# A two-layer decoder trunk on one core: where the token statistics are transposed, and when the relative-bias table is made

## The chip, the cores and the metric

The kernel runs on 1 core of one Trainium2 chip. The metric is device time in microseconds (us); the kernel before takes 1341.06 us, the median of 3 runs (1340.65 to 1341.84).

## The reference

512 tokens of width 1024 pass through two layers. In short:

```python
hn = rmsnorm(h, norm_mix_g[i])
h = h + mixer(hn)            # layer 0: stick-breaking and differential heads; layer 1: dilated attention
h = h + square(relu(rmsnorm(h, norm_mlp_g[i]) @ w_mlp_up[i])) @ w_mlp_down[i]
h = h + (p[i] @ w_ple_proj[i]) * sigmoid(rmsnorm(h, norm_ple_g[i]) @ w_ple_gate[i])
```

Two parts of the mixers matter here. `rmsnorm` divides each token by the root of its mean square, so every query, key and value of a token carries one factor for that token. And the softmax heads (the differential ones of layer 0 and all of layer 1) add a bias that depends on the distance of query and key alone: `table[t5_bucket(rel)]`, from a table of 32 buckets by 16 heads.

## The kernel before, in words

**Tiling.** The activations lie transposed, as eight tiles `h[k]` of 128 features by 512 tokens. Every fp32 operand is split into a high and a low part, and each product is three matmuls (`mm3`, lines 129 to 131). ScalarE (ACT) makes the high part of weights (L120); GpSimd (POOL) or VectorE (DVE) makes the low part (L121).

**One mixer.** Heads come in four groups; layer 0 takes them in the order 2, 3, 0, 1, the first two being differential heads. `project(g)` (L389) makes a group's queries, keys and values. For the first group of a layer (`start`) it runs `queries_keys()` and then `values()`; for later groups the values come first. `attend` (L529) runs in steps that `interleave` (L150) places between the units of the next group's `project`.

**The first group.** Queries are contracted first (two accumulators, "mm" banks of PSUM), then key block 0 (an "mm" bank) and key block 1 (an "sc" bank). After key block 0 `statistics()` (L373) finishes the token statistics: two matmuls with a matrix of ones (L237, L238), then `rsqrt` (L192) on ACT and DVE, whose last step (L199) gives `rstd`, a tile that holds each token's factor along its columns. `tok_cols` (L257) turns it into one column per 128 tokens: four transposes on TensorE (PE; L260) and one DVE instruction (L262) that writes `rcol`. Then the held queries and the keys are evacuated (`evacuate`, L448): each takes one DVE product with `rstd` (L451) into the single "tmp" buffer, ACT copies (L457, L465, L466) and DVE differences (L458, L467). `values()` fills two PSUM banks, one "sc" and one "tp", with 96 matmuls in two halves, and `evacuate_values` (L412) scales them by `rcol` (ACT L421, DVE L422).

**The table.** `prepare()` (L301) is called once, after the first `project` of layer 0 (L625). It takes four "e" tiles and the "tmp" tile, loads the table, a 0/1 matrix and offsets by six transfers (L304 to L309) and the lambda vectors by one (L312, into "tmp"), multiplies the table in two pieces (PE L316, each into a fresh one of the two "sc" banks), joins the offsets (four DVE instructions, L318) and writes the result to device memory (`urow`, four transfers, L319). Five small DVE and ACT instructions (L320 to L325) make the lambda factor. `load_bias` (L488) reads `urow` (L491) at the start of a differential head or a dilated head, and `soft` (L494) adds it to the scores by a DVE instruction (L499).

**What sets the order.** The program text gives each instruction its dependencies and its rank; the order on each engine's queue is fixed at build time by a planner, which lets an engine take the highest-ranked instruction that it holds to be ready. So an engine's order differs from the text: the transposes (L260), which the text puts ahead of key block 1, stand in the trace between that block's 17th and 18th matmul, and the loads of the next group (L112) stand ahead of the table's. At run time each queue keeps that order and waits where an operand is late.

Of the kernel before, what the change touches and what calls it, by code (L numbers as in the profile page):

```python
# [62 lines left out]
def trunk(  # L63
# [8 lines left out]
    def nm(s):  # L72
        uid[0] += 1
        return f"{s}_{uid[0]}"
# [13 lines left out]
    def t2k(tag, pool=None, dtype=F32):  # L88
        return (pool or spool).tile([P, S], dtype, tag=tag, name=nm(tag), bufs=T_BUFS.get(tag, 2))
# [6 lines left out]
    def ps(tag):  # L96
        return psum.tile([P, S], F32, tag=tag, name=nm(tag), bufs=PS_BUFS[tag])
# [4 lines left out]
    def ps_wide():  # L102
        t = ps(wide[wide_i[0] % 8])
        wide_i[0] += 1
        return t
# [4 lines left out]
    def wload(src):  # L110
        raw = wpool.tile([P, src.shape[-1]], F32, tag="raw", name=nm("raw"), bufs=2)
        nc.sync.dma_start(raw, src)  # L112
        return raw

    def wsplit(raw, i, nk, n, pool=None):
        bufs = 3 if pool is None else 4
        hi = (pool or wpool).tile([P, nk, n], F32R, tag="wh", name=nm("wh"), bufs=bufs)
        lo = (pool or wpool).tile([P, nk, n], F32R, tag="wl", name=nm("wl"), bufs=bufs)
        src = raw[:, i * nk * n:(i + 1) * nk * n].rearrange("p (k c) -> p k c", k=nk)
        nc.scalar.activation(hi, src, AF.Copy)  # L120
        lo_eng[0].tensor_tensor(lo, src, hi.bitcast(F32), op=ALU.subtract)  # L121
        return hi, lo

    def block(src, nk, n):
        raw = wload(src)
        return [wsplit(raw, i, nk, n) for i in range(src.shape[-1] // (nk * n))]

    def mm3(acc, lh, ll, rh, rl, start, stop):
        nc.tensor.matmul(acc, lh, rh, start=start, stop=False)  # L129
        nc.tensor.matmul(acc, lh, rl, start=False, stop=False)  # L130
        nc.tensor.matmul(acc, ll, rh, start=False, stop=stop)  # L131
# [69 lines left out]
    def use_tables(after):  # L201
        ins = nc.scalar.preload_act_table_set("natural_log_exp_and_others").ins
        for a in after:
            order(ins, a)
        return ins
# [51 lines left out]
    def tok_cols(rstd):  # L257
        rp = ps("tp")
        for t in range(QT):
            nc.tensor.transpose(rp[:, t * P:(t + 1) * P], rstd[:, t * P:(t + 1) * P], ident)  # L260
        rc = spool.tile([P, QT], F32, tag="rcol", name=nm("rcol"), bufs=2)
        nc.vector.tensor_scalar(rc, rp.rearrange("p (t c) -> p t c", c=P)[:, :, 0], -0.5, None, op0=ALU.mult)  # L262
        return rc
# [96 lines left out]
    def mixer(layer, norm, nxt):  # L360
# [10 lines left out]
        stat = {}  # L371

        def statistics():  # L373
            if not layer:
                for k in range(KT):
                    norm.stats(k, last_split)
            stat["rstd"] = norm.finish(use_tables(sig_tail) if layer else None)
            stat["rcol"] = tok_cols(stat["rstd"])

        nblk = [0]  # L380

        def next_block():
            nblk[0] += 1
            return w_in[layer, nblk[0] - 1]
# [4 lines left out]
        def project(g, cur):  # L389
            kind = "dil" if layer else ("sb" if g < 2 else "diff")  # L390
            start = not first
            first.append(g)
            v = mpool.tile([P, QT, 512], F32R, tag="v", name=nm("v"), bufs=2)

            def values():
                raw = wload(next_block())
                banks = [ps_wide() if start else ps("mm") for _ in range(QT // 2)]
                accs = [b[:, c:c + 256] for b in banks for c in (0, 256)]
                for half in range(2):
                    wh, wl = wsplit(raw, half, 4, 256)  # L400
                    for t in range(QT):
                        for k in range(4):
                            ah, al = ahl[4 * half + k]
                            tk = slice(t * P, (t + 1) * P)
                            mm3(accs[t], ah[:, tk], al[:, tk], wh[:, k], wl[:, k],
                                half == 0 and k == 0 and t % 2 == 0, half == 1 and k == 3 and t % 2 == 1)
                            yield 1.0
                        if half == 1 and t % 2 == 1:
                            evacuate_values(t - 1, accs[t - 1])
                            evacuate_values(t, accs[t])  # L410

            def evacuate_values(t, acc):  # L412
                sc = stat["rcol"][:, t:t + 1]
                if kind == "diff":
                    src = acc
                    vh, vl = v[:, t, 0:256], v[:, t, 256:512]
                else:
                    src = acc.rearrange("p (a c) -> p a c", a=4)
                    vv = v[:, t, :].rearrange("p (a b c) -> p a b c", a=4, b=2)
                    vh, vl = vv[:, :, 0, :], vv[:, :, 1, :]  # L420
                nc.scalar.activation(vh, src, AF.Copy, scale=sc)  # L421
                nc.vector.scalar_tensor_tensor(vl, src, sc, vh.bitcast(F32), op0=ALU.mult, op1=ALU.subtract)  # L422

            heads = []

            def queries_keys():
                qscale = -0.5 * HD ** -0.5 if kind == "sb" else 0.5 * HD ** -0.5
                qk, waiting = [], []
                for isq in (True, False):
                    src = next_block()  # L430
                    lo_eng[0] = nc.vector if start else nc.gpsimd
                    blk = blk0 if isq and start and not layer else block(src, KT, P)
                    lo_eng[0] = nc.gpsimd
                    accs = [ps_wide() if start else ps("mm") for _ in range(2)]
                    if start and isq:
                        yield from lin_units(accs, blk, ahl, 0, KT, True)
                        waiting = accs
                        continue
                    for i, acc in enumerate(accs):
                        yield from lin_units([acc], [blk[i]], ahl, 0, KT, False)  # L440
                        if waiting:
                            statistics()
                            for x, held in enumerate(waiting):
                                evacuate(True, x, held, qk, qscale)
                            waiting = []
                        evacuate(isq, i, acc, qk, qscale)

            def evacuate(isq, i, acc, qk, qscale):  # L448
                rstd = stat["rstd"]
                f = t2k("tmp")  # L450
                nc.vector.scalar_tensor_tensor(f, acc, qscale if isq else -0.5, rstd, op0=ALU.mult, op1=ALU.mult)  # L451
                lower, upper = slice(0, 64), slice(64, 128)
                if isq:
                    qq = []
                    for a, b in ((lower, upper), (upper, lower)):
                        q = mpool.tile([P, S], F32R, tag="qq", name=nm("qq"), bufs=6)
                        nc.scalar.activation(q[a], f[a], AF.Copy)  # L457
                        nc.vector.tensor_tensor(q[b], f[a], q[a].bitcast(F32), op=ALU.subtract)  # L458
                        qq.append(q)
                    qk.append(qq)  # L460
                else:
                    for s, (a, b) in enumerate(((lower, upper), (upper, lower))):
                        kl = klz[s][kl_i[0] % KLB]
                        kh = mpool.tile([P, S], F32R, tag="kh", name=nm("kh"), bufs=5)
                        nc.scalar.activation(kh[a], f[a], AF.Copy)  # L465
                        nc.scalar.activation(kh[b], f[a], AF.Copy)  # L466
                        nc.vector.tensor_tensor(kl[a], f[a], kh[a].bitcast(F32), op=ALU.subtract)  # L467
                        heads.append((qk[i][s], kh, kl))
                    kl_i[0] += 1
            cur.extend((g, kind, v, heads))  # L470
            if start:
                wide_i[0] = 0
                yield from queries_keys()
                yield from values()
            else:
                yield from values()
                yield from queries_keys()
# [144 lines left out]

        cur = []
        run(project(groups[0], cur))
        if layer == 0:  # L625
            prepare()
        for n, g in enumerate(groups[1:]):
            steps = attend(*cur)
            cur = []
# [253 lines left out]
```

## Time and profile before

| | |
|---|---|
| Median of 3 runs | 1341.06 us (1340.65 to 1341.84) |
| Profiled execution | 1337.92 us, span 1336.1 us |
| PE busy | 1300.5 us, 97% of the span |
| DVE busy | 817.4 us, 61% |
| ACT busy | 632.2 us, 47% |
| POOL busy | 164.4 us, 12% |
| Mean granted clock of PE | 0.998 |

Busy time is the union of an engine's instructions. PE's is near the whole span, but matmuls overlap in the pipe, so what it could save is read from its waits and from the chain of work that ended last. The span is 1.8 us shorter than the execution's own time, which is 3.14 us under the median.

### The profile page before, as it was taken

How to read it: one execution, taken by the hardware profiler on the slowest of the kernel's cores; microseconds unless marked ns; L12 is line 12 of the kernel's file. 1: busy time of each engine (PE TensorE's matmuls, PEld its weight loads, DVE VectorE, ACT ScalarE, POOL GpSimd, SP SyncE). 2: the span in 40 equal slices, each digit the busy share in tenths (PEclk: the TensorE clock that was granted, in tenths of full speed). 3: DMA queues.
4: the chain of work that ended last, by engine and by line, in shares of the span. 5: the costliest groups of instructions: out<-in, count | busy, mean ns of one | idle time of the engine just before them, and what ended most of it. 6: DMA issues, size and time to landing. Idle time of an engine off the chain costs nothing.

```text
span 1336.1 us, 16330 instructions
## 1 busy us (share of the span) xinstructions
PE 1300.5 (97%) x6360; PEld 1088.8 (81%) x6360; DVE 817.4 (61%) x1389; ACT 632.2 (47%) x1085; POOL 164.4 (12%) x90
## 2 busy tenths in 40 slices
PE   8999999899999999999999999999999999999997
PEld 6878777688888888888888898888888888888886
DVE  6788789865344344345667888887644434434566
ACT  5576758554223232233456666775422313324344
POOL 2322332310000000000003222221000000000001
PEclk9999999999999999999999999999999999999999
DMA  6321322243233222222232232213322232322221
GB/s 217 109 89 56 119 87 103 88 158 98 101 104 104 98 95 95 95 95 95 95 119 87 76 112 74 72 64 133 119 95 95 98 103 103 105 96 95 95 79 64
DMA packets 28030, 133.06 MB, mean 100 GB/s; under 512 B 3312, under 2 KB 4048, under 8 KB 15280
## 3 DMA queue, kind: packets, MB, share of 16 engines
q1 hardware_dynamic: 27952, 132.01, 29.0%
q8 instruction: 50, 0.82, 0.2%
q14 instruction: 28, 0.23, 0.1%
HBM read 125.63 MB, written 6.37 MB: 99 GB/s over the span
## 4 chain that ended last, share of the span: by engine, by line
PE 75%; DVE 14%; ACT 7%; issue 2%; DMA 0%; SPq 0%; ACTq 0%
PE mm L130 11%; PE mm L129 11%; PE mm L131 11%; PE tp L129 5%; PE tp L131 5%; PE tp L130 5%; PE sc L129 5%; PE sc L131 5%; PE sc L130 5%; PE pv L130 2%; PE pv L129 2%; PE pv L131 2%; DVE qq L458 2%; DVE e L563 2%; PE pv L525 2%
## 5 line engine op out<-in xcount | busy, mean ns | idle before, releaser
L120 ACT ACTIVATE wh<-raw 128x1024 fp32r<-128x1024 f32 (+1 forms) x216 | 224.7, 1043 | 496.8 <-PE mm L130 178.4
L129 PE MATMUL mm<-hi,wh 128*128 128x512 f32 x564 | 226.2, 401 | 0.5 <-ACT hi L169 0.5
L130 PE MATMUL mm<-lo,wh 128*128 128x512 f32 x564 | 220.5, 391 | 0.6 <-DVE lo L170 0.6
L131 PE MATMUL mm<-hi,wl 128*128 128x512 f32 x564 | 220.4, 391 | 0.3 <-DVE wl L121 0.3
L121 DVE TENSOR_TENSOR wl<-raw,wh 128x1024 fp32r<-128x1024 f32 x150 | 183.4, 1224 | 44.1 <-ACT wh L120 37.8
L121 POOL TENSOR_TENSOR wl<-raw,wh 128x1024 fp32r<-128x1024 f32 (+1 forms) x66 | 153.8, 2331 | 348.7 <-ACT wh L120 320.6
L131 PEld LDWEIGHTS mm<-hi,wl 128*128 128x128 f32 x564 | 105.9, 188 | 23.4 <-DVE wl L121 0.8
L129 PEld LDWEIGHTS mm<-hi,wh 128*128 128x128 f32 x564 | 106.2, 188 | 21.3 <-ACT hi L169 1.3
L130 PEld LDWEIGHTS mm<-lo,wh 128*128 128x128 f32 x564 | 106.2, 188 | 20.2 <-DVE lo L170 1.3
L502 ACT ACTIVATE e<-e,mn 128x128 f32<-128x128 f32 (+3 forms) x96 | 53.9, 561 | 51.5 <-DVE mn L499 50.8
L130 PE MATMUL mm<-ul,wh 128*128 128x512 f32 x192 | 74.7, 389 | 0.0
L131 PE MATMUL mm<-uh,wl 128*128 128x512 f32 x192 | 74.7, 389 | 0.0
L129 PE MATMUL mm<-uh,wh 128*128 128x512 f32 x192 | 74.7, 389 | 0.0
L131 PE MATMUL sc<-hi,wl 128*128 128x512 f32 x168 | 65.6, 390 | 0.0
L130 PE MATMUL sc<-lo,wh 128*128 128x512 f32 x168 | 65.4, 389 | 0.0
L129 PE MATMUL sc<-hi,wh 128*128 128x512 f32 x168 | 65.4, 389 | 0.0
L129 PE MATMUL mm<-wh,hi 128*128 128x256 f32 (+1 forms) x216 | 65.4, 303 | 0.0
L130 PE MATMUL mm<-wl,hi 128*128 128x256 f32 (+1 forms) x216 | 64.1, 297 | 0.4 <-DVE wl L121 0.4
L131 PE MATMUL mm<-wh,lo 128*128 128x256 f32 (+1 forms) x216 | 63.8, 295 | 0.0
L675 DVE TENSOR_TENSOR h<-h,mm 128x512 f32<-128x512 f32 x24 | 16.5, 688 | 72.7 <-PE mm L131 72.7
L129 PE MATMUL tp<-hi,wh 128*128 128x512 f32 x152 | 59.1, 389 | 0.0
L130 PE MATMUL tp<-lo,wh 128*128 128x512 f32 x152 | 59.1, 389 | 0.0
(218 smaller groups left out, 2835.1 us busy)
## 6 DMA issues: line engine op xcount, KB each, us to landing
raw<-in_w_up_dram SPq DMA_DIRECT2D x32, 1024.0 KB, 4.9
raw<-in_w_down_dram SPq DMA_DIRECT2D x32, 1024.0 KB, 4.9
raw<-in_w_in_dram SPq DMA_DIRECT2D x23, 1024.0 KB, 4.9
raw<-in_w_gate_dram SPq DMA_DIRECT2D x8, 1024.0 KB, 4.9
bias<-urow SPq DMA_DIRECT2D x24, 256.0 KB, 3.2
raw<-in_w_outa_dram SPq DMA_DIRECT2D x8, 768.0 KB, 4.3
pjd<-tmp SPq DMA_DIRECT2D x16, 256.0 KB, 2.2
pj<-pjd SPq DMA_DIRECT2D x16, 256.0 KB, 4.8
```

Source lines behind the costliest of these rows:

```text
L120: nc.scalar.activation(hi, src, AF.Copy)
L121: lo_eng[0].tensor_tensor(lo, src, hi.bitcast(F32), op=ALU.subtract)
L129: nc.tensor.matmul(acc, lh, rh, start=start, stop=False)
L130: nc.tensor.matmul(acc, lh, rl, start=False, stop=False)
L131: nc.tensor.matmul(acc, ll, rh, start=False, stop=stop)
L458: nc.vector.tensor_tensor(q[b], f[a], q[a].bitcast(F32), op=ALU.subtract)
L502: nc.scalar.activation(e[:, 0:n], e[:, 0:n], AF.Exp, scale=-1.0, bias=mn, accum_out=s)
L525: nc.tensor.matmul(op[:, q0:S], stat(j), mov, start=c == 0, stop=c == nmm - 1)
L563: nc.vector.tensor_tensor_scan(kr, kr, kr, 1.0, op0=ALU.mult, op1=ALU.bypass)
L675: nc.vector.tensor_tensor(h[2 * c + i], h[2 * c + i], acc, op=ALU.add)
```

## The change

Three edits. `tok_cols` leaves `statistics()` and is called in `values()` of a layer's first group, when the second half of the value weights has been split and before that half's matmuls (in both layers). `prepare()` leaves its place after the first `project` and is called in that `project` of layer 0, between `queries_keys()` and `values()`. No instruction is added or taken away.

```diff
@@ statistics
             stat["rstd"] = norm.finish(use_tables(sig_tail) if layer else None)
-            stat["rcol"] = tok_cols(stat["rstd"])
@@ values
                 for half in range(2):
                     wh, wl = wsplit(raw, half, 4, 256)
+                    if start and half == 1:
+                        stat["rcol"] = tok_cols(stat["rstd"])
                     for t in range(QT):
@@ project
                 yield from queries_keys()
+                if not layer:
+                    prepare()
                 yield from values()
@@ mixer
         run(project(groups[0], cur))
-        if layer == 0:
-            prepare()
         for n, g in enumerate(groups[1:]):
```

## Rows read from the trace of the kernel before

**Rows 1.** The page: busy time of each engine with its share of the span, and the shares of the chain that ended last by engine.

```profile
PE 1300.5 (97%) x6360; PEld 1088.8 (81%) x6360; DVE 817.4 (61%) x1389; ACT 632.2 (47%) x1085; POOL 164.4 (12%) x90
...
PE 75%; DVE 14%; ACT 7%; issue 2%; DMA 0%; SPq 0%; ACTq 0%
```

**Rows 2.** PE's waits over the whole span: engine, tile and line that waited, the instruction that ended the wait, then us in total, times, longest.

```profile
PE sc L484 <- DVE mn L499: 5.0, 4, 1.8
...
PE tp L260 <- DVE rstd L199: 3.2, 2, 2.0
PE sc L316 <- DVE v L422: 1.9, 1, 1.9
...
PE sc L484 <- DVE v L422: 0.9, 1, 0.9
```

**Rows 3.** The chain that ended last, layer 0, from the statistics to the second group's values: start us, us, what.

```profile
30.96 0.70 DVE rstd L199
31.69 0.70 DVE tmp L451
32.41 0.64 ACT qq L457
33.08 0.69 DVE qq L458
...
46.08 0.69 DVE klz L467
46.81 0.49 DVE v L422
...
47.83 0.49 DVE v L422
48.37 0.39 PE sc L316 x2
```

**Rows 4.** The timeline of PE around the transposes of layer 0 and around the table's products: start us, us, engine, line, operation, out<-in, count, and in brackets the idle time before and what ended it.

```profile
29.29 0.39 PE L130 MATMUL sc<-lo,wh 128*128 128x512 f32 x1
31.71 0.66 PE L260 MATMUL tp<-ident,rstd 128*128 128x128 f32 x4 [2.03 <-DVE rstd L199]
32.12 0.48 PE L131 MATMUL sc<-hi,wl 128*128 128x512 f32 x1
...
45.41 1.03 PE L316 MATMUL sc<-e,e 32*16 32x512 f32 x2
...
48.69 0.39 PE L129 MATMUL mm<-wh,hi 128*128 128x256 f32 x1
```

**Rows 5.** The same place in layer 1: two pieces of the chain, then four rows of PE's timeline.

```profile
706.30 0.70 DVE tmp L451
...
722.45 0.50 DVE v L422
...
704.81 0.39 PE L130 MATMUL sc<-lo,wh 128*128 128x512 f32 x1
706.33 0.65 PE L260 MATMUL tp<-ident,rstd 128*128 128x128 f32 x4 [1.13 <-DVE rstd L199]
...
721.87 0.28 PE L131 MATMUL mm<-wh,lo 128*128 128x256 f32 x1
723.08 0.36 PE L484 MATMUL sc<-kh,qq 128*128 128x256 f32 x1 [0.93 <-DVE v L422]
```

**Rows 6.** The timeline of DVE, layer 0.

```profile
32.40 0.16 DVE L262 TENSOR_SCALAR rcol<-tp 128x4 f32<-128x4 f32 x1
...
42.14 0.69 DVE L451 SCALAR_TENSOR_TENSOR tmp<-sc,rstd 128x512 f32<-128x512 f32 x1
...
48.62 1.27 DVE L318 SCALAR_TENSOR_TENSOR e<-sc,e 16x512 f32<-16x512 f32 x2
...
50.21 0.47 DVE L318 SCALAR_TENSOR_TENSOR e<-sc,e 16x128 f32<-16x128 f32 x2
...
55.18 0.29 DVE L499 CUSTOM_DVE_ANT_0 e<-sc,bias 128x128 f32<-128x128 f32 x1 [2.51 <-PE mm L131]
```

**Rows 7.** The queue of SP, layer 0; then the landing time of the 0/1 matrix's load (KB each, median us from issue to landing) and of the first three loads of the bias.

```profile
30.53 0.41 SPq L305 DMA_DIRECT2D e<-in_onehot_dram  x1
...
46.84 0.35 SPq L312 DMA_DIRECT2D tmp<-in_lambdas_dram  x1
...
51.88 1.29 SPq L491 DMA_DIRECT2D bias<-urow  x3
...
e<-in_onehot_dram SPq DMA_DIRECT2D x1, 64.0 KB, 5.3
...
DMA to landing us min/median/max: 3.2/3.5/3.6
```

**Rows 8.** Busy time by stretch: us, then each engine's busy us and instructions, the granted clock of PE, the DMA share and GB/s.

```profile
29.30:32.10 2.80, 0.77 (x6) 0.40 (x5) 2.70 (x4) 0.00 (x0) 0.35 (x1) 1.00 0.52 120
45.40:48.70 3.30, 1.37 (x6) 0.23 (x5) 2.70 (x6) 1.94 (x5) 0.10 (x1) 1.00 0.62 194
60.00:75.00 15.00, 15.00 (x86) 12.51 (x85) 13.15 (x45) 11.52 (x29) 5.05 (x2) 1.00 0.29 100
75.00:130.00 55.00, 50.38 (x291) 43.18 (x289) 47.05 (x112) 36.45 (x80) 14.96 (x7) 1.00 0.23 70
1330.00:1333.00 3.00, 0.00 (x0) 0.00 (x0) 1.90 (x6) 2.27 (x6) 0.00 (x0) 0.55 0.40 157
```

## The prediction, made before the changed kernel was run

> **What bounds the kernel now.** I read the page first: PE is busy 97% of the span, but the chain that ended last runs on PE for 75%, on DVE for 14% and on ACT for 7% [rows 1]. So there are stretches where PE works and yet does not set the end, and a wait of PE in such a stretch is worth nothing by itself. Then PE's waits: the transposes wait for the statistics twice, 3.2 us in total, and the table's second product waits 1.9 us [rows 2]. These two are what the change touches. Last the chain through that place: the reader is to see that from `rstd` (done at 31.66) it goes through DVE and ACT, query by query and key by key, to the second value evacuation (47.83 to 48.32), and comes back to PE only at the table's second product, 48.37 [rows 3]. The transposes are not on it. Layer 1 has the same chain, from the first evacuation at 706.30 to the second value evacuation at 722.45; there PE waits 0.93 us for that very instruction [rows 5].
>
> **The change part by part.**
>
> *The transposes, layer 0.* PE stops after the matmul of 29.29; matmuls follow each other there every 0.23 us, so the next could start at 29.52 and starts at 32.12: 2.60 us, 2.03 of it idle and 0.41 the transposes themselves [rows 4]. Without them key block 1 (7 matmuls left, 1.6 us) ends at 31.2 instead of 33.8. The 96 value matmuls fill 33.8 to 45.41, 0.12 us each, 11.6 us together; with the 0.41 of the transposes put back among them they end at 31.2 + 11.6 + 0.41 = 43.2. The transposes then find `rstd` long done, so no wait replaces the old one. But the values' evacuation needs ACT and DVE, and these stand in the chain above until 46.81 whatever PE does [rows 3]. The DVE instruction that moves along (0.16 us at 32.40) lies in a gap in which DVE waits for ACT's copy, 32.41 to 33.05 [rows 3, 6]. **Worth on the end: 0**, bounds 0 and -0.16.
>
> *The transposes, layer 1.* The same: the next matmul could start at 705.04 and starts at 706.74 (transposes at 706.33, 0.41 us), so PE gains 1.70 - 0.41 = 1.29 us. It then meets the wait at 723.08, which ends with the DVE chain: 0.93 becomes 2.2 us [rows 5]. Worth 0, same bounds.
>
> *The table: what is queued where.* Its loads stand on SP's queue from 30 us, already ahead of the values' work, because SP takes what is ready, not what the text lists first; the 0/1 matrix lands at 30.53 + 5.3 = 35.83 [rows 7]. The value weights were loaded before that, so I expect none of these to move, and SP to hold nothing back. The lambda load needs the single "tmp" buffer, so it stays behind the last key difference (46.77), at 46.84; what queues behind it on SP are the writes of the table and the bias loads [rows 7]. If they do not pass it, the bias cannot start loading before 47.2. POOL gets no new instruction.
>
> *The table on PE.* The products cost 1.03 us and 48.69 - 48.37 = 0.32 us [rows 3, 4]. Each needs one of two "sc" banks: one holds key block 1 until the DVE product of 42.14 ends at 42.83 [rows 6], the other the first two value blocks until 48.32 [rows 3]. In the kernel before, the second product stands at the head of PE's queue after the values, so the second group's values cannot start before 48.69, though nothing else holds them [rows 4]. Layer 1, without a table, shows the same place free of it: its values end at 706.74 + 1.6 + 11.6 = 719.95, and by 722.0 PE has done 2.0 us of the next group before it has to wait [rows 5]. So at the moment when the chain lets go (48.32), layer 0 can be 2.0 + 0.32 = **2.3 us** ahead of before.
>
> *The table on DVE.* The four additions take 1.27 + 0.47 = 1.74 us, and lie at 48.62 to 50.68, behind the chain [rows 6]. Moved ahead, they may fall into the gaps of the chain (cost 0) or lengthen it (1.74). The chain's gaps are waits for ACT like the one of 0.5 us above, and an addition of 0.67 us does not quite fit one, so I put two thirds on the chain: 1.2 us. PE's lead is then 2.3 - 1.2 = 1.1 us; its ends are 2.3 and 0.6.
>
> *The bias.* From the end of the additions to the first use of the bias are 55.18 - 50.68 = 4.5 us (issue at 51.88, landing 3.2 us later) [rows 6, 7]. With the additions done by 48.6 at the latest if they stand before the value evacuations, the bias lands at 53.1, 2 us earlier. DVE is idle before 55.18 [rows 6], so attention starts that much earlier.
>
> *Sum.* From 60 to 75 us PE is busy 15.00 of 15.00, so there its lead of 1.1 us is kept. From 75 to 130 it is busy 50.4 of 55, 4.6 us of gaps, mostly waits for DVE [rows 2, 8]; DVE's 2 us absorb some. DVE is busy 47 of 55 there, near its own limit, so I count 0.5 us, between 0 and 2. Total 0 + 0 + 1.1 + 0.5 = 1.6 us. Against the profiled execution's own 1337.92 (span 1336.1) that is 1336.3 (span 1334.5); it lies 3.14 under the median of the runs, 1341.06, so as a median **1339.5 us**.
>
> **The rivals.**
>
> *A, faster: both leads hold.* The additions fit into the gaps, PE gains 2.3, and DVE's earlier start takes 2 us out of the waits between 75 and 130. For it: the bias is the only thing DVE waits for at 55.18. Against it: DVE's load after 75. 1341.06 - 4.3 = 1336.8 us; at the most 2.3 + 4.6 = 6.9 us.
>
> *B, slower: the first product stands among the value matmuls and waits there.* The planner places it where it holds the bank to be free; the chip's chain is later than such a plan wherever an instruction runs long. PE's queue is in order, so every value matmul behind the product waits too. The bank comes free at 42.83; with n value matmuls behind it, the second group starts at 42.83 + 1.35 + 0.12 n. That equals 48.69 at n = 38, and above it this decides: n = 60 gives 51.4, 2.7 us late. At the head of the values (n = 96) it can have the other bank and waits for its operand: 35.83 + 1.35 + 11.6 + 0.41 = 49.2, 0.5 us late. For it: the transposes stand where `rstd` was 2.03 us late [rows 4], so the plan does run ahead of the chip here. Against it: the earlier bias pays some back. Time 1341.7 to 1343.8, taken as 1343.
>
> [...]
>
> *C, the change does not do what it says.* The planner could leave the products behind the values, since it places by readiness. Then only the transposes move: 1341.0 us.
>
> **How the numbers follow.** Forecast case 0.46, A 0.27, B 0.15, C 0.12. A measurement of this kernel can tell about 0.2%, 2.7 us, from no change. Faster than that (under 1338.4): nearly all of A and the far end of the forecast case, 0.30. Slower (over 1343.7): the far end of B with the clock, 0.12. Within: 0.58. The range reaches from A's deeper part, 1335.0, to B's n of 60 less a little, 1343.5.
>
> **What would show it.** Right: no wait of L260; value matmuls from about 31.2; PE's waits for L422 grown in layer 1 from 0.9 to about 2 us, and its span from there on unmoved; L316 ahead of the second group's values without the 1.9 us; the first L499 near 53. Wrong: a wait of L316 for L451 or for L305's load with value matmuls behind it (B); value evacuations in layer 0 that start well before 46.8, which would mean that the chain is not fixed; or a change of more than 1 us after layer 1 has begun.

## The result and the profile after

The changed kernel takes **1344.6 us** (median of 15 runs), the kernel before 1341.0 in the same session: ratio 1.0022, with a 95% interval of 1.0013 to 1.0031. It is slower, by 3.6 us by the medians and by 2.9 by the ratio: its runs fall into two groups, ten at 1342.3 to 1345.4 us and five at 1340.5 to 1341.0, and the median lies in the upper one. The prediction was 1339.5 us, its range ended at 1343.5. Of all the runs below one is slow, a run of x5 with 2005.57 us at a mean clock of 0.603, which is left out of its ratio.

The profiled execution of after took 1344.91 us (span 1343.1); that of before took 1337.92, less than its median run. The two traces are therefore 7.0 us apart where the medians are 3.6 apart; where that comes from is told below. In the code of after the lines from 401 on stand one to three further down: 484 is 487, 499 is 502, 422 is 423, 592 is 595.

The page of after, its busy times and the shares of the chain, answers [rows 1]:

```profile
PE 1305.4 (97%) x6360; PEld 1093.9 (81%) x6360; DVE 819.7 (61%) x1389; ACT 632.0 (47%) x1085; POOL 164.0 (12%) x90
...
PE 73%; DVE 14%; ACT 8%; issue 2%; DMA 1%; POOL 0%; SPq 0%; ACTq 0%; POOLq 0%; DVEq 0%
```

The work is the same, and yet PE is busy 4.9 us longer, at the same instruction count. So something slowed the matmuls themselves. PE's waits, answering [rows 2]:

```profile
PE sc L487 <- DVE mn L502: 4.9, 5, 1.3
PE pv L594 <- ACT tmp L591: 4.6, 2, 2.4
...
PE sc L487 <- DVE v L423: 2.3, 1, 2.3
PE sc L316 <- DMA e<-in_onehot_dram: 2.0, 1, 2.0
```

The transposes' wait (L260, 3.2 us) is gone from the list, as intended, and so is the 1.9 us ahead of the table's second product. In their place stand three others: 4.6 us ahead of the normalisation's ones-matmuls, 2.3 for the value evacuation of layer 1 (0.9 in before), and 2.0 for the load of the 0/1 matrix. The last one in PE's timeline of layer 0, answering [rows 4]:

```profile
30.64 0.39 PE L131 MATMUL sc<-hi,wl 128*128 128x512 f32 x1
30.87 0.28 PE L129 MATMUL tp<-wh,hi 128*128 128x256 f32 x1
...
33.02 0.28 PE L129 MATMUL tp<-wh,hi 128*128 128x256 f32 x1
35.29 1.01 PE L316 MATMUL sc<-e,e 32*16 32x512 f32 x2 [1.99 <-DMA e<-in_onehot_dram]
...
48.05 0.28 PE L129 MATMUL mm<-wh,hi 128*128 128x256 f32 x1
```

Key block 1 ends at 30.87 and the values begin without a stop. After 19 of the 96 value matmuls comes the table's first product, whose operand is still on its way. The chain of waits now runs through that load, not through DVE (compare [rows 3]):

```profile
30.25 4.91 DMA e<-in_onehot_dram
...
35.29 1.01 PE sc L316 x2
```

Behind it the first value evacuation waits for PE, while in before ACT came to it (45.52) straight from its key copies:

```profile
48.01 0.47 ACT L422 ACTIVATE v<-sc,rcol 128x256 fp32r<-128x256 f32 x1 [1.33 <-PE sc L131]
```

The granted clock by stretches: start:end, us, then busy time and count of PE, PE loads, DVE, ACT and POOL, then the clock, the DMA share and GB/s (the same columns as in [rows 8]). The first two are the stretch after that product, then come the wait ahead of line 594 and the stretch behind it, then the wait of layer 1 and the stretch behind it:

```profile
37.00:40.00 3.00, 3.00 (x16) 3.00 (x16) 2.94 (x5) 0.47 (x1) 0.00 (x0) 0.50 0.05 12
40.00:44.00 4.00, 4.00 (x32) 3.65 (x32) 3.03 (x8) 3.02 (x6) 0.00 (x0) 0.97 0.11 32
98.00:101.50 3.50, 1.02 (x4) 0.29 (x2) 1.30 (x2) 2.77 (x5) 0.00 (x0) 1.00 0.41 173
101.70:105.10 3.40, 3.40 (x12) 3.02 (x13) 0.99 (x4) 2.43 (x4) 0.61 (x1) 0.50 0.00 0
726.00:729.70 3.70, 1.40 (x12) 1.29 (x11) 2.50 (x8) 2.43 (x7) 0.53 (x1) 1.00 0.84 281
729.80:733.10 3.30, 3.30 (x17) 3.30 (x16) 2.77 (x9) 1.09 (x4) 1.76 (x1) 0.50 0.02 7
```

Three times the clock falls to 0.50 soon after PE stood for 2.0 to 2.4 us, and in these stretches PE is slower: from 38.06 us on the value matmuls follow each other every 0.21 us, where they took 0.12 before the product. One wait of that length, 2.17 us ahead of line 594 at 85 us, is not followed by a low stretch (1.00 from 85.8 to 101 us). In before's trace the clock is 1.00 in every stretch between 28 and 1330 us.

Layer 1, answering [rows 5]: the end of the chain, then the last row of it in PE's timeline.

```profile
726.78 0.50 DVE v L423
727.30 0.48 ACT v L422
727.81 0.49 DVE v L423
```

```profile
728.44 0.35 PE L487 MATMUL sc<-kh,qq 128*128 128x256 f32 x1 [2.30 <-DVE v L423]
```

SP's queue, answering [rows 7], and DVE's first use of the bias, answering [rows 6]:

```profile
30.25 0.41 SPq L305 DMA_DIRECT2D e<-in_onehot_dram  x1
...
38.93 3.12 SPq L319 DMA_DIRECT2D urow<-e  x4
42.62 1.29 SPq L494 DMA_DIRECT2D bias<-urow  x3
45.73 0.33 SPq L312 DMA_DIRECT2D tmp<-in_lambdas_dram  x1
```

```profile
49.82 0.28 DVE L502 CUSTOM_DVE_ANT_0 e<-sc,bias 128x128 f32<-128x128 f32 x1
```

The additions do not lengthen the chain, the bias loads pass the lambda load, and the first use of the bias comes 5.4 us earlier than in before. All this is as the change would have it, and it is not paid out.

**Where the 7.0 us between the traces lie.** The same work in both kernels, cut where ACT begins the first value evacuation of layer 0's third group, of layer 1's first and of its second group. The rows of before, then of after:

```profile
28.00:112.83 84.83, 76.12 (x481) 66.05 (x480) 67.10 (x148) 51.17 (x106) 26.20 (x11) 1.00 0.29 95
...
720.14:731.78 11.64, 10.71 (x87) 10.40 (x86) 8.73 (x25) 7.23 (x18) 4.55 (x2) 1.00 0.35 112
731.78:1330.00 598.22, 592.71 (x2891) 497.67 (x2889) 360.01 (x667) 273.05 (x480) 60.12 (x29) 1.00 0.27 93
```

```profile
28.00:118.05 90.05, 79.28 (x480) 69.49 (x479) 69.05 (x148) 50.75 (x107) 25.39 (x11) 0.96 0.26 88
118.05:725.56 607.51, 597.17 (x2816) 496.04 (x2815) 362.52 (x517) 279.71 (x448) 66.66 (x32) 1.00 0.29 101
725.56:738.67 13.11, 10.81 (x75) 10.49 (x75) 8.77 (x25) 7.24 (x18) 4.52 (x2) 0.87 0.34 102
738.67:1337.00 598.33, 592.76 (x2891) 497.67 (x2889) 360.21 (x667) 273.17 (x480) 60.20 (x29) 1.00 0.27 93
```

Up to the third group after needs 90.05 - 84.83 = 5.22 us more. Of these PE is busy 79.28 - 76.12 = 3.16, which the clock explains ((1 - 0.96) x 90.05 = 3.6), and idle 10.77 - 8.71 = 2.06. Layer 1's start takes 13.11 - 11.64 = 1.47 more, at a mean clock of 0.87; (1 - 0.87) x 13.11 = 1.7. The rest adds 0.3 us. So some two thirds of what the traces lose are matmuls at half clock, and the waits themselves are 2.06 us. (In layer 1 the longer wait is not a loss of its own, since PE had done 12 matmuls more ahead of it: 75 are left in after's stretch, 87 in before's.)

### The profile page after: what moved, and what is told of

It is laid out like the page before. It is cut to its first block, busy times and chain, and to the rows that moved or that the text cites. A ratio compares the mean times of both kernels' runs of the same rounds, so it can differ in the third digit from the quotient of the medians.

```text
span 1343.1 us, 16331 instructions
## 1 busy us (share of the span) xinstructions
PE 1305.4 (97%) x6360; PEld 1093.9 (81%) x6360; DVE 819.7 (61%) x1389; ACT 632.0 (47%) x1085; POOL 164.0 (12%) x90
## 4 chain that ended last, share of the span: by engine, by line
PE 73%; DVE 14%; ACT 8%; issue 2%; DMA 1%; POOL 0%; SPq 0%; ACTq 0%; POOLq 0%; DVEq 0%
PE mm L130 11%; PE mm L129 11%; PE mm L131 11%; PE tp L130 5%; PE tp L131 5%; PE tp L129 5%; PE sc L131 5%; PE sc L130 5%; PE sc L129 5%; PE pv L130 2%; PE pv L131 2%; PE pv L129 2%; DVE qq L459 2%; DVE e L566 2%; DVE e L567 1%
```

## The experiments

Every run's mean granted clock is on record, and over the 102 runs of before that accompany the experiments time goes with it: median 1338.3 us at a clock of 0.998 (13 runs), 1339.3 at 0.997 (19), between 1340.7 and 1341.2 at 0.996 to 0.994 (64), 1342.4 at 0.993 (6). Before's median run, then, has low stretches that its profiled run has not. Of after, the five runs at 0.997 or 0.998 take 1340.5 to 1341.0, the nine at 0.994 or less 1342.3 to 1345.4. So at the same mean clock the change still costs 1.2 to 2.3 us where the clock is high, and 3.8 by the medians at 0.994: the mean clock alone does not account for its price. The theory tested is that the change joins or makes waits of PE and the clock falls after them (theory 1); the rival is in each case that the order of the steps costs the time and low stretches come by chance. All ratios are to before in the same session (its median 1340.4 to 1341.0); the runs come from several sessions on different chips, so kernels of different sessions compare better by their ratios than by their medians.

| kernel | median us | ratio to before | 95% interval |
|---|---|---|---|
| the change | 1344.6 | 1.0022 | 1.0013 to 1.0031 |
| x1 transposes alone | 1341.61 | 1.0012 | 1.0004 to 1.0021 |
| x2 table alone | 1342.54 | 1.0016 | 1.0007 to 1.0024 |
| x3 transposes, layer 1 alone | 1342.36 | 1.0008 | 0.9999 to 1.0017 |
| x4 change, own tiles | 1341.52 | 1.0007 | 0.9999 to 1.0016 |
| x5 change, normalisation later | 1344.44 | 1.0026 | 1.0016 to 1.0037 |
| x6 before, y*y on ScalarE | 1335.43 | 0.9957 | 0.9945 to 0.9969 |
| x7 = x3 with nine matmuls in the wait | 1340.96 | 0.9999 | 0.9991 to 1.0008 |
| x9 = x4 with x5's and x6's edits | 1335.41 | 0.9958 | 0.9946 to 0.9970 |
| x10 change, y*y on ScalarE | 1336.11 | 0.9968 | 0.9955 to 0.9980 |
| x12 x10's edit, normalisation alone | 1341.29 | 1.0007 | 0.9998 to 1.0016 |
| x13 x10's edit, statistics alone | 1340.72 | 1.0006 | 0.9997 to 1.0015 |
| x15 before, eight matmuls in a wait | 1342.56 | 1.0019 | 1.0010 to 1.0028 |
| x16 = x6 with the same eight | 1338.26 | 0.9988 | 0.9980 to 0.9997 |
| x17 = x4 with x7's nine | 1341.55 | 1.0011 | 1.0002 to 1.0020 |

**x1, the transposes alone.** Both layers; the table stays behind the values.

```
-            stat["rcol"] = tok_cols(stat["rstd"])
...
+                    if start and half == 1:
+                        stat["rcol"] = tok_cols(stat["rstd"])
```

> Only the column transposes are moved, in both layers; the relative-bias table stays in its old place. Theory 1 (two short waits of TensorE merge into one longer one, and the clock falls to half after it): in layer 0 the wait of 2.03 us ahead of the transposes is gone and the wait ahead of the first table product grows from 1.9 to about 4 us, in layer 1 the wait ahead of the first score grows from 0.93 to 2.2-2.3 us; behind each stands a stretch of some 3.4 us at a granted clock near 0.5 that costs about 1.5-1.7 us. Total 1342.5 to 1344.5 us where the kernel before takes 1341.0, mean clock 0.995 or less. Theory 2 (the extra time of the full change is the new order of layer 0 alone, low-clock stretches come and go by chance): the same two waits, no more low stretches than the kernel before has, 1341.0 us within 0.7.

PE's waits in x1, and the stretch of layer 1:

```profile
PE sc L316 <- DVE v L423: 4.2, 1, 4.2
...
PE sc L485 <- DVE v L423: 2.3, 1, 2.3
```

```profile
721.35:734.41 13.06, 10.75 (x75) 10.44 (x75) 8.83 (x25) 7.24 (x18) 4.50 (x2) 0.87 0.32 101
```

Two waits of 2.03 and 1.93 became one of 4.2; 1.13 and 0.93 became 2.3. PE gains nothing by it, and the clock falls in both layers (a mean of 0.98 from 28 to 113.98 us, and the 0.87 of the row). 0.9 us slower by the medians, 1.6 by the ratio. The waits and the low stretches are as theory 1 says; the median of 1341.61 is below its range and still within theory 2's, so the time alone does not decide between them.

**x2, the table alone** (`prepare()` between keys and values, the transposes as before).

> Only the table is moved between keys and values; the transposes stay ahead of the K projection's second block. Theory 1: the wait of 2.0 us ahead of the transposes stays, so the table's products reach TensorE some 2 us later and their operand has landed (wait below 0.5 us instead of 1.99); no low stretch of the clock at 37-40 us; the attention of layer 0's first two groups still loses 3 to 5 us against the kernel before between 80 and 113 us, with waits of about 2 us ahead of the ones-matmuls at line 592 (L591/592 of before) and a low stretch near 102; layer 1 as before, wait 0.9. Total 1342.5 to 1344.5 us. Theory 2 (the loss in layer 0's attention comes from the low stretch and the front's shift, not from the table's place): 1341.0 us within 0.7.

The product in PE's timeline, then PE's waits:

```profile
37.33 1.03 PE L316 MATMUL sc<-e,e 32*16 32x512 f32 x2
```

```profile
PE pv L593 <- ACT tmp L590: 3.5, 2, 2.4
```

The first product comes 2.0 us later than in after and finds its operand landed; no wait. The waits ahead of the ones-matmuls (line 593 there) come with the table's move alone, 1.2 and 2.4 us. The clock falls at 33 us, behind the 2.0 us wait that before has as well, which theory 1 had not expected: from 32.99 us on 128x512 matmuls follow each other every 0.42 us, for 0.23 ahead of it. The mean clock of 0.96 from 28 to 116.75 us means, by an estimate, some 7 us at half clock; these leave room for the stretch expected near 102 us too. 1.9 us slower: the table's part is about half of the change's price, and with x1 the two parts make up 2.8 of the 3.6 us (by the ratios 2.1 and 1.6 against 2.9).

**x3, the transposes of layer 1 alone.**

> Only layer 1's column transposes are moved. Theory 1: the wait ahead of the first score in layer 1 is 2.2-2.3 us instead of 0.93, the 1.13 us wait ahead of the transposes is gone, and behind the longer wait stands a stretch of about 3.4 us at half the clock that costs 1.5 us: 1342.0 to 1343.0 us against 1341.0, the difference standing wholly behind 725 us. Theory 2 (low stretches are chance): 1341.0 within 0.5, no low stretch behind that wait in the profile.

```profile
727.01 0.35 PE L487 MATMUL sc<-kh,qq 128*128 128x256 f32 x1 [2.31 <-DVE v L425]
```

```profile
728.00:731.30 3.30, 3.30 (x17) 3.30 (x16) 2.97 (x8) 1.00 (x5) 2.10 (x1) 0.50 0.07 27
44.00:48.60 4.60, 2.96 (x19) 1.90 (x17) 3.90 (x4) 3.18 (x8) 2.03 (x1) 1.00 0.33 91
48.80:55.50 6.70, 6.61 (x30) 6.20 (x31) 3.78 (x11) 1.40 (x3) 2.38 (x1) 0.50 0.60 199
```

The wait and the low stretch of layer 1 are as theory 1 says; from the first to the second group's values it takes 13.10 us where before takes 11.64. The last row is the other lesson of this run: layer 0's order is here that of before, and the clock falls behind before's own 1.9 us wait at 48 us, which it did not in before's profiled run. Neither theory said that it would come and go, and the mean clock of 0.94 from 28 to 116.72 us leaves, by an estimate, 3 to 5 us at half clock beside the 6.7 of that row, so the difference is not wholly behind 725 us as theory 1 had it. With the interval touching 1 the median alone decides nothing; the stretch of layer 1 does, here, in x7 and in x12.

**x7, x3 with nine 128x512 matmuls in layer 1's wait.**

```
+                if layer and start:
+                    junk = ps("mm")
+                    for j in range(9):
+                        nc.tensor.matmul(junk, ones_r, ahl[0][0], start=j == 0, stop=j == 8)
```

> The kernel with layer 1's transposes alone moved, plus nine 128x512 matmuls (about 2 us, results unused) between the last value matmul and the first score of layer 1. Theory 1 (the 2.3 us wait there drops the clock, and the drop costs 1.5 us): the wait falls below 0.5 us, no low stretch near 728-733 us, layer 1's second group of values starts where the kernel before starts it (11.6 us behind the first, not 13.1), total about 1341.0 us, 1.0 to 1.7 us less than without the matmuls. Theory 2 (low stretches do not come from that wait): the low stretch stays and the total is as without them or 0.3 us more.

```profile
720.28 2.25 PE L417 MATMUL mm<-hi,ones_r 128*128 128x512 f32 x9
...
724.80 0.35 PE L491 MATMUL sc<-kh,qq 128*128 128x256 f32 x1 [0.25 <-DVE v L429]
```

```profile
721.90:733.81 11.91, 11.66 (x94) 11.26 (x92) 7.71 (x25) 7.03 (x19) 4.23 (x2) 1.00 0.31 100
```

Two microseconds of useless work take the place of the wait, the clock stays at 1.00, and the stretch is 1.19 us shorter; the median is 1.4 below x3's (in another session; by the ratios 1.2, and the intervals overlap). Two kernels told of below settle it without added work. x12 and x5 have the wait of layer 1 too, and their clock stayed at 1.00. The rows of x12, with the same 75 matmuls as after's 13.11 us:

```profile
726.40 0.36 PE L490 MATMUL sc<-kh,qq 128*128 128x256 f32 x1 [2.31 <-DVE v L426]
```

```profile
723.50:735.09 11.59, 9.28 (x75) 8.97 (x75) 8.68 (x25) 7.24 (x18) 4.54 (x2) 1.00 0.35 115
```

The stretch takes 11.59 us in x12 and 11.37 in x5, as in before (11.64), and 13.06 to 13.11 in the four profiles where the clock fell (a mean of 0.87). This shows it for layer 1: the joined wait costs nothing by itself, the half clock behind it costs 1.5 us.

**x4, the change with the table's operands in tiles not used yet** (`prepare(oT[0:4])` for four tiles of "e"), so that their loads go out earlier.

> The changed kernel, but the table's four operand tiles are ones that nothing has used yet, so their loads are issued right behind the K block's load and not at 30.2 us. Theory 1: the first table product finds its operand landed (wait below 0.3 us instead of 1.99), no low stretch at 37-40 us, the second group of values starts 0 to 0.7 us earlier than the 48.05 of the changed kernel; what is lost between 80 and 113 us (about 5 us) and in layer 1 (1.5 us) stays. Total 1343.5 to 1345 us. Theory 2 (the low stretch at 37 us sets what is lost later): the loss of 80-113 us shrinks to under 2 us, 1341 to 1342 us.

```profile
36.11 0.39 PE L316 MATMUL sc<-o 32*16 32x128 f32 x2 [1.71 <-DVE o L318]
```

The wait for the load is gone, but the second product then waits 1.7 us for the bank that the first pair of additions empties, and the clock still falls: from 38.04 us on the value matmuls follow each other every 0.21 us, for 0.12 ahead of the wait. The time is theory 2's, the mechanism is not: from the second group's first value evacuation to the third's it takes 54.72 us (after 55.19, before 53.70), so the loss behind the front has hardly shrunk. The gain stands ahead of it, at layer 0's first value evacuation (46.13 for 48.01 us), and is kept to the end. The late load was worth some 2 us of the change's price (by the ratios too), more than theory 1 allowed.

**x5, the change with the normalisation one step later** (`m -= 2` for `m -= 1`).

> The changed kernel with the differential heads' normalisation (lines 586 to 597) issued one attend step later. Theory 1 (the table's move made ScalarE's copy at line 591 late, so TensorE stands about 2.2 and 2.4 us ahead of the ones-matmul at line 594, and the clock then falls near 102 us for 3.4 us, worth 1.3-1.5 us): both waits shrink below 0.5 us, no low stretch between 95 and 110 us, the first K evacuation of group 1 (106.13 us in the changed kernel) comes 3 to 5 us earlier, total 1340.0 to 1341.5 us against 1344.6. Theory 2 (those waits only stand where other waits of the same steps would stand, VectorE being behind): the waits reappear ahead of line 487 or 513 and the total stays within 1 us of 1344.6.

```profile
98.92 0.75 PE L594 MATMUL pv<-tmp,ones_r 128*128 128x512 f32 x1 [2.30 <-ACT tmp L591]
...
151.88 0.50 PE L594 MATMUL pv<-tmp,ones_r 128*128 128x512 f32 x1 [2.20 <-ACT tmp L591]
```

The time stays: theory 1 fails here. Of the two waits one stays; the other, at 85 us in after, is gone, but a new one of 2.20 us stands at 151.88. The matmul behind the first takes 0.75 us for 0.50, and the mean clock from 28 to 116.11 us is 0.96. The third group begins 1.9 us earlier than in after (116.11 for 118.05), and layer 1 0.5 us later (726.08 for 725.56). In after it is not PE that is early at the first of the waits, it is ACT's copy that is late, since ACT waits before it, for DVE:

```profile
80.97 0.72 ACT L505 ACTIVATE e<-e,mn 128x512 f32<-128x512 f32 x1 [3.49 <-DVE mn L502]
...
85.29 0.50 PE L594 MATMUL pv<-tmp,ones_r 128*128 128x512 f32 x1 [2.17 <-ACT tmp L591]
```

**x6, before with y*y on ScalarE.** This takes the longest DVE instruction out of the chain that leads to [rows 3]. The line serves ten products of 128x512, six of the statistics and four of the heads' normalisation.

```
-        nc.vector.tensor_tensor(t, y, y, op=ALU.mult)
+        nc.scalar.activation(t, y, AF.Square)
```

> The kernel before with the product y*y of the statistics (line 197) made by ScalarE's Square and not by VectorE, where the 128x512 product takes 2.71 us in layer 0's chain. Theory 1 (the DVE-ACT chain from the statistics to the value evacuation sets PE's waits in both layers): rstd is ready about 2 us earlier in layer 0 and 1 us in layer 1, the waits of 2.03 and 1.13 us ahead of the transposes shrink below 0.5 us, those ahead of the first table product and of layer 1's first score do not grow, total 1337.0 to 1339.0 us against 1341.0. Theory 2 (the chain is not what sets the end, or later waits take the gain up): 1340.0 to 1341.5 us.

The first line is before's DVE, the next two are ACT and DVE of x6:

```profile
27.49 2.71 DVE L197 TENSOR_TENSOR e<-rstd 128x512 f32<-128x512 f32 x1 [2.46 <-ACT rstd L196]
```

```profile
27.28 0.63 ACT L197 ACTIVATE e<-rstd 128x512 f32<-128x512 f32 x1
...
27.95 0.69 DVE L198 SCALAR_TENSOR_TENSOR e<-tp,e 128x512 f32<-128x512 f32 x1 [3.15 <-ACT e L197]
```

5.35 us faster, the best version with x9 and more than theory 1 said. A wait of PE can be had back by making its cause shorter (0.63 for 2.71 us) where moving what waits gave nothing. The 5.35 us are not the price of that wait alone, since the edit covers the other nine products too: in the profiles x6 leads before by 1.3 us at the first value evacuation, and by 2.8 at layer 1's. The waits left are 0.55 (L260), 1.93 (L316) and, in layer 1, 0.93.

**x9 and x10, combinations.** x9 puts the edits of x4, x5 and x6 together, x10 is the change with x6's edit.

> The changed kernel with three edits together: the table's operands in tiles nothing has used (loads early), the normalisation one step later, y*y on ScalarE. Theory 1 (each removes one of the waits found): waits ahead of the table products and of line 594 below 0.5 us, layer 1's wait ahead of the first score 1.2 us instead of 2.3, at most one low stretch, 1335 to 1338 us. Theory 2 (another engine, VectorE in layer 0's attention, holds the steps): 1339 to 1342 us.

> The changed kernel with y*y of the statistics and of the normalisation on ScalarE. Account so far: time = the matmuls' own time + TensorE's waits + half of the low-clock stretches. Theory 1 (the change's price is waits plus low stretches, which a shorter chain shrinks): layer 1's wait falls from 2.3 to 1.2 us and its low stretch goes, the waits ahead of line 594 fall as the normalisation's inputs come earlier, the wait for the 0/1 matrix's load stays near 2 us; 1336.0 to 1338.5 us, still 0.5 to 3 us above the 1335.4 of the kernel before with the same edit. Theory 2 (the chain's saving adds to both alike): 1339.0 to 1340.0 us, 5.3 us below the 1344.6 of the changed kernel.

x9 shows no low stretch between 28 and 108.81 us (1.00) and no wait ahead of line 594; x10 keeps 2.17 us for the load, 1.3 ahead of line 594 and, as expected, 1.14 in layer 1 without a low stretch (1.00). With the shorter chain the change costs 1336.11 against 1335.43, 0.7 us by the medians (1.5 by the ratios) and not 3.6: most of its price hangs on waits that the edit shortens. x9 only equals x6, so in these runs nothing of the change is worth keeping.

**x12 and x13, x10's edit in halves.** x12 has it in the heads' normalisation alone, x13 in the statistics alone.

> The changed kernel with y*y on ScalarE in the heads' normalisation alone (not in the statistics). Theory 1 (VectorE's backlog in layer 0's attention makes the inputs of line 594 late; the 128x512 product of 0.7 to 2.4 us is part of it): the waits of 2.17 and 2.39 us shrink by 1 us or more together, layer 1's wait stays 2.3 us with its low stretch; 1341.5 to 1343.0 us against 1344.6. Theory 2 (the waits come from the new order of the steps, not from that product): waits within 0.4 us of 2.17 and 2.39, 1343.5 to 1344.6 us.

> The changed kernel with y*y on ScalarE in the statistics alone. Theory 1 (start of the layers and attention are paid apart): layer 1's wait 1.2 us instead of 2.3 and no low stretch behind it, the waits of 2.17 and 2.39 us ahead of line 594 stay; 1339.0 to 1341.5 us. Theory 2 (what the attention loses follows from the late start of layer 0): those waits shrink below 1 us together and the time is that with the edit in both places, 1336 to 1337 us.

In x12 one of the two waits (2.39 at 101 us) goes, the other stays at 2.11; in x13 the second stays at 2.40, the first falls to 1.23, and layer 1's falls to 1.15. Theory 1 in the main, though x12's 1341.29 us lie just below its range and x13's first wait shrank: 3.3 and 3.9 us off the change by the medians, 7.2 together where x10 has 8.5 (by the ratios 2.0 and 2.1 where x10 has 7.2, so the halves do not simply add). The second wait goes when the normalisation's products leave DVE. For the first one the runs show that it comes with the table's place (1.16 us in x2) and that DVE is late, but not which instruction makes it so. x12's wait in layer 1 is 2.31 us and its clock stays at 1.00 there, as in x5: of the six profiles with that wait at 2.3 us the clock fell in four (0.87 in layer 1's stretch).

**x15, x16, x17, more matmuls in waits.** x15 and x16 put eight ahead of the first table product, x17 nine into layer 1's wait of x4.

> The kernel before with eight 128x512 matmuls (1.8 us, results unused) issued ahead of the first table product, in the wait of 1.93 us that TensorE has there. Theory 1 (that wait is where the kernel before loses the clock in most of its runs, seen at 47.5 to 48.7 us in the profiles of four kernels whose order there is that of before): no low stretch near 48 us, 1338.5 to 1340.0 us against 1341.0. Theory 2 (the matmuls only take the place of the wait and low stretches come elsewhere): 1341.0 us within 0.5.

> The kernel before with y*y on ScalarE and the same eight matmuls ahead of the first table product. Theory 1: what the low stretch at 47.5 us costs the kernel with y*y on ScalarE goes, 1333.3 to 1334.5 us (that kernel: 1335.4 median, 1333.6 in its run at clock 0.999). Theory 2: 1335.4 within 0.5.

> The changed kernel with the table's operands in tiles that nothing has used and nine matmuls in layer 1's wait ahead of the first score. Theory 1: the low stretch near 728 us goes and with it 1.0 to 1.6 us, 1339.8 to 1340.6 us where the same kernel without the nine matmuls took 1341.5. Theory 2: 1341.5 within 0.4.

x15 and x16 failed, 2 to 3 us slower than without. The low stretch at 48 us is gone, as theory 1 says, but the planner now put all four additions behind the lambda product, which waits for a load; the first scores, 13 matmuls into the second group's values, need the additions' bank:

```profile
51.63 1.66 DVE L318 SCALAR_TENSOR_TENSOR e<-sc,e 16x512 f32<-16x512 f32 x4
...
53.04 0.36 PE L484 MATMUL sc<-kh,qq 128*128 128x256 f32 x1 [2.97 <-DVE e L318]
```

Behind this wait the clock falls in x15 (from 54.30 us on the value matmuls follow each other every 0.21 us, for 0.12 ahead of it), but not in x16 (1.00 from 28 to 113.89 us), whose wait is as long. So they tell nothing of the clock's price at the old wait. x17 took layer 1's stretch from 13.10 to 11.89 us in its profile, yet its median is that of x4: by the time, theory 2. Nine of x4's eleven runs have a mean clock of 0.997 or 0.998, its profiled run 0.994, so its median run had perhaps no low stretch there to save; that is argued, not shown, and x17's own runs do not lie higher (0.994 to 0.998).

## Why the prediction was wrong

*What bounds the kernel.* Right for the order of before: the chain through DVE and ACT sets the end in both layers (x6 shortens it and gains, x1 moves PE's work and does not). In layer 0 of the changed kernel it no longer held: DVE's last key difference ends at 45.66 us, 1.1 earlier than in before, and the first value evacuation then waits 1.33 us for PE (48.01 for 45.52), which lost its time at the load and at half clock.

*The transposes.* Their waits came out as worked out: none at L260, 2.2 forecast in layer 1 and 2.30 measured. "Worth on the end: 0, bounds 0 and -0.16" is **the first step that failed**: it priced a wait by its length alone. Layer 1's, joined to 2.3 us, was followed by a fall of the clock in four of six profiles, worth 1.47 us in layer 1's stretch (13.11 for 11.64; 1.52 by x12, 1.19 by x7). The bounds left that out although the chances count the clock for B. Nor is a shorter wait shown to be safe: the profiled run of before kept its clock through 2.03 and 1.93 (1.00 in [rows 8]) where x2 lost it behind the one (from 32.99 us) and x3 behind the other (0.50 from 48.8 us), as did x6 (0.21 us between 128x256 matmuls at 47.81, for 0.12) and, by its mean of 0.98 from 28 to 114.36 us, probably x7.

*The table on PE.* **The second step that failed** is "I expect none of these to move, and SP to hold nothing back": the loads did not move, the product did, from 45.41 to where PE came to it at 33.3 (35.29 - 1.99), and its operand landed at 35.16. This is rival B near the head of the values, with 77 matmuls behind it, waiting for its operand as B said; it had a chance of 0.15 and a price of 0.5 to 2.7 us. The lead at the second group's values is 48.69 - 48.05 = 0.64 us, within the ends of 0.6 to 2.3. Without the wait and the low clock (1.99, and an estimated 1.5 as in layer 1) it would have been 4.1.

*The table on DVE, the bias.* The additions found gaps and cost the chain nothing; the bias was 5.4 us early where I said 2, since its loads passed the lambda load.

*Sum.* **The third step that failed**: +0.5 from waits absorbed between 75 and 130. Attention ran ahead only until about 80 us. PE is idle 2.06 us more up to the third group, with two new waits ahead of line 594 that x2 gives to the table's move. DVE was named there as near its own limit; that the table's move would make the normalisation late was in no rival. That it does so by the earlier bias, which changes the order of DVE's and ACT's queues, is likely but not shown: no run moves the bias alone.

*The signs.* Two of the signs of being wrong came: L316 waited for L305's load with value matmuls behind it, and from layer 1's first value evacuation on after takes 1.6 us more.

*The clock.* After the wait of 1.99 us for a transfer the row 37:40 shows 0.50; in the four other kernels with that wait (x5, x10, x12, x13) the mean clock from 28 us to the third group is 0.96, 0.98, 0.96 and 0.94. The traces show the same 0.50 after waits for ACT (2.39 us) and DVE (2.30), and 1.00 after others as long (2.17 us at 85 us, 2.31 in x12). The forecast put no price on this. The chance of 0.12 for a slower result did, with "the far end of B with the clock": no run shows that term, since in none does PE wait for the load as long as from 31.2 to 35.83. In its place the runs showed 3 us at 0.50 behind the 1.99, by an estimate 1.5 us (half of the 3).

## What to carry to other kernels

Work that is moved off a stall joins this wait to the next one if the same chain ends both (1.13 and 0.93 us became 2.3); before moving it, ask what ends the second wait, and shorten that instead. A wait of PE had two prices here, its length and, in some executions, the matmuls at half clock behind it (1.5 us in layer 1), and one profiled run without the second does not show that it is absent: before's profiled run has a mean clock of 0.998, 70 of its 102 runs 0.996 or less. An operation that is issued earlier must have its loads issued earlier too (the product stood 1.99 us for the 0/1 matrix), and an early result (the bias, by 5.4 us) may change the order of the queues behind it, which no run here shows alone.

## What the runs showed that I had not expected

The product y*y of 128x512 on DVE takes 2.71 us at 27.49 and 0.68 at 88.59 in the same kernel; the first starts while POOL's split (24.80 to 29.65) runs and ends at 30.20, 0.55 behind it. In x6 the next product of two SBUF tiles, `rstd`, takes 1.29 for 0.69 us in the same place and ends 0.55 behind the split (29.96 for 29.41), while ACT does y*y there in 0.63 us beside the same split. In before at 99.73 us y*y takes 2.50 us beside a split that ends 0.55 us ahead of it. Two more differences on before's chain end in the same way, 0.55 and 0.56 us behind a split: `qq` at 35.91 (1.96 us) and `klz` at 43.58 (2.48), where such an instruction takes 0.69 without a split beside it. In after no split runs beside that `klz` (0.69 us at 43.67), which is part of why its chain ends earlier. What delays these instructions no run shows, nor what it would be worth to keep the splits away from the chain.

A low clock is not always paid: over before's 102 runs time rises by 0.26 us for each us of it (low time taken as twice 1 less the mean clock, times the span), not 0.5. Part of it may lie where DVE's chain sets the end anyway; no run shows that.
